# S5 mixer: the latent's norm ahead of all context states, T's loads behind the latent's operands on the DMA queue, and a new share-out of the output copies

## The chip, the cores and the metric

One core of one Trainium2 chip runs the program. The metric is the device time of one execution in microseconds; lower is better. Every time below is in microseconds unless marked ns. Engines: PE multiplies matrices, DVE and ACT do elementwise work and copies, POOL (GpSimd) helps with copies, SP issues nearly all DMA transfers.

## The reference, cut to what matters

Two layers work on 512 latent tokens `x` and 256 context tokens `ctx`, each 1024 wide, in float32. Layer 0 has an S5 mixer (a diagonal state space model in both directions, 64 groups of 16 channels and 64 states), layer 1 a GLA mixer. The context runs first and its last state starts the latent's scan.

```
for i in range(DEPTH):                                        # DEPTH = 2
    x  = ffn_half_step(x,  ...);  xc = ffn_half_step(xc, ...)
    hx = rmsnorm(x,  norm_w[i, 1]) * (1.0 + sx[4]) + sx[3]
    hc = rmsnorm(xc, norm_w[i, 1]) * (1.0 + sc[4]) + sc[3]
    yc, yx = s5_mixer(hc, hx, ...) if i == 0 else gla_mixer(hc, hx, ...)
    x = x + sx[5] * yx
    x = ffn_half_step(x, ...)                                 # and xc alike, but for the last layer
return rmsnorm(x, final_norm_w)

# s5_mixer, for each direction (backward on the flipped tokens), u = h in groups:
bu = einsum('blgc,gpc->blgp', u, bbar)                        # complex: real and imaginary half
h[t] = abar * h[t - 1] + bu[t]
y = einsum('blgp,gcp->blgc', h_re, c_re) - einsum('blgp,gcp->blgc', h_im, c_im)
# then, from both directions:
z = einsum('bld,de->ble', gelu(y_f + y_b + d_skip * h), w_glu) + b_glu
val, gate = split(z);  out = val * sigmoid(gate)
```

## The kernel before, in words

Tokens stand in the columns of transposed tiles (`xT`, 128 channels by 768 tokens, eight channel tiles `kt`). Context comes first (256 columns), then the latent (512). The code calls operations in a program order, and a planner inside the tile framework then fixes each engine's order at build time. It weighs what it expects of durations and of buffers coming free, so an edit in one place can move rows elsewhere too. On the chip each engine and each DMA queue works strictly in its order and waits by semaphores. `c.tc.issue_after(ins)` keeps what is called under it behind the named instruction.

The S5 mixer takes time in steps of 8 tokens (`L5`), so that a scan needs 32 steps for the context (`NX5`) and 64 for the latent, 96 (`N5`) in all:

- **Norm and operands.** `norm` sums squares, takes the reciprocal root on DVE (`rstd`, sums on PE at L163, small steps at L167 to L175), spreads it over the partitions on PE (`spread`, L182), scales on DVE (L201) and shifts on ACT (L788). It runs in thirds of 256 tokens. Its last third is the latent's second half. Parts of a norm are put into a queue (`later`) and let go one after the other by `tick()`, or all at once by `ensure()`. When the latent's last third is done, `put` stores it to DRAM (`s5U<-big`), and `load_u` reads it back in groups (`u<-s5U`), the operand of the states.
- **States** (`states`, matmuls at L816, evacuation at L821 by ACT or DVE). For each `kt` the operand R (tiles `rm`, and the weight slots `wraw`, `whi`, `wlo`) is multiplied by `u`. The context's matmuls have 32 columns, the latent's 64. R is stored in the weight slots that later loads use again.
- **Scan** (`scan`, L504, on DVE): two directions, for each step a product with the diagonal and two additions. The first context steps follow the context states; then latent states and scan steps are called in turn.
- **Lagged part** (`lagged`): for each `kt` a tile of T is loaded (`c.dma` at L849) into a free weight slot, reordered by ACT (L850) and multiplied by `u` on PE (L856); ACT writes the result back over `u` (L858).
- **Outputs** (`outputs`). For each `kt` the scanned states are gathered into `xs` (two buffers, by `kt % 2`): for each of two group halves four sorts of copies (L890), forward and backward, real and imaginary. A forward copy is 64 x 380 elements; a backward one comes as 64 x 124 (context) and 64 x 256 (latent) on DVE. The table at the call in `work` says which engine takes which: `copies[z][a]`, z the direction and a the half. In kt 0 and 1 the first 80 steps are copied early by ACT, and only the rest by the table. PE multiplies `xs` with the operand (L911), DVE adds the lagged part (L913), ACT applies gelu (L915); the result goes to DRAM (`s5Y`).
- **GLU** (`glu`): the result is read back (`yk`, three buffers), split into a high and a low part (`h`; ACT cast L936, DVE difference L937), and multiplied by the weights, which are split too (L88 on ACT, L89 on DVE; the three products are L113, L114 and L115). It alternates between two weights at the start, and it is followed by feed-forward layers made of the same products.

The calls in order, in `hybrid_trunk`: load the context's u and R, context states (in the loop a `tick()` each, and `ensure()` at kt 3), first scan steps, a modulation block (`ten`), latent states in turn with scan steps, the rest of the scan, `lagged`, another block, `outputs`, two blocks, the outputs' `work`, `glu`.

Of the kernel before, what the change touches and what calls it, by code (L numbers as in the profile page):

```python
# [15 lines left out]
P = 128  # L16
# [11 lines left out]
def fview(t, off, dims, p0=0, n=P):  # L28

    b = t[p0:p0 + n]  # L30
    return bass.AP(b.tensor, b.offset + off, [list(b.ap[0])] + [list(d) for d in dims])


def dview(ap, off, dims):

    return bass.AP(ap.tensor, ap.offset + off, [list(d) for d in dims])
# [432 lines left out]
C5 = 16  # L469
S5P = 64  # L470
L5 = 8
N5 = TOK // L5
# [4 lines left out]
class S5:  # L477
# [285 lines left out]
    def load_u(self, kt, kind):  # L763

        tile = (self.u[kt][:, :, :NX5], self.u[kt][:, :, NX5:])[kind]
        n = tile.shape[-1]
        self.c.dma(tile, dview(self.U[kind], kt * P * L5 * n, [(n, P), (C5 * L5 * n, 8), (1, n)]))

    def inputs(self):

# [30 lines left out]
    def states(self, kt, kind, evac):  # L801


        c, nc, r = self.c, self.c.nc, self.r
        n0, n = ((0, NX5), (NX5, N5 - NX5))[kind]
        m = (32, 64)[kind]
        u = self.u[kt][:, :, n0:n0 + n]
        banks = [c.bank() for _ in range(kind + 1)]
        for part in range(2):
            for z in range(2):  # L810
                i = (part * 2 + z) * 4 * n
                b, o = banks[i // 512], i % 512
                for q in range(4):
                    for g in range(2):
                        for p0 in range(64 * g, 64 * g + 64, m):
                            nc.tensor.matmul(b[p0:p0 + m, o + q * n:o + (q + 1) * n],  # L816
                                             self.rm[2 * kt + part][:, z * 512 + q * P + p0:z * 512 + q * P + p0 + m],
                                             u[:, 2 * q + g], start=True, stop=True)
                src = fview(b, o + z * (n - 1), [(n, 4), (1 - 2 * z, n)])
                dst = fview(r, n0 * P + part * 64 + z * 32 + 4 * kt, [(1, 4), (P, n)])  # L820
                last = (nc.scalar.copy if evac[part] else nc.vector.tensor_copy)(out=dst, in_=src)  # L821
        return last
# [20 lines left out]
    def lagged(self):  # L843

        c, nc = self.c, self.c.nc
        for kt in range(KT):
            tm = c.spare()
            c.dma(tm.rearrange("p (i x) -> p i x", i=L5), self.T[:, :, kt * P:(kt + 1) * P])
            tg = c.spare().rearrange("p (x i) -> p x i", i=L5)  # L849
            nc.scalar.copy(out=tg.rearrange("p x i -> p i x"), in_=tm.rearrange("p (i x) -> p i x", i=L5))  # L850
            for h in range(2):
                b = c.bank()
                u = self.u[kt][:, 4 * h:4 * h + 4]
                for i in range(4):
                    g = 4 * h + i
                    nc.tensor.matmul(b[:, i * N5:(i + 1) * N5], tg[:, g * C5:(g + 1) * C5].rearrange("p c i -> p (c i)"),  # L856
                                     u[:, i], start=True, stop=True)
                nc.scalar.copy(out=u.rearrange("p g n -> p (g n)"), in_=b[:, :4 * N5])  # L858

    def outputs(self, pool, ahead, yp, last):  # L860


        c, nc, r = self.c, self.c.nc, self.r
        loaded, self.ys = {}, []

        def load(kt):
            om = [c.spare() for _ in range(2)]
            for z in range(2):
                c.dma(om[z], self.O[kt][z])
            return om  # L870
        for kt in range(ahead):
            loaded[kt] = load(kt)
        xs = [pool.tile([P, 2, 8, N5], F32, name=f"xs{i}", tag=f"xs{i}", bufs=1) for i in range(2)]
        for x in xs:
            nc.gpsimd.memset(x[:, 0, :, 0:1], 0.0)
        def states(kt, s0, s1, copies):

            x = xs[kt % 2]
            nc.gpsimd.memset(x[:, 1, :, NX5 - 1:NX5], 0.0)
            for g in range(2):  # L880
                for a in range(2):
                    def move(z, lo, hi, to, step):

                        lo, hi = max(lo, s0), min(hi, s1)
                        if lo >= hi:
                            return
                        at, to = (lo, to(lo)) if step > 0 else (hi - 1, to(hi - 1))
                        src = fview(r, at * P + a * 64 + z * 32 + 4 * kt, [(1, 4), (step * P, hi - lo)], 64 * g, 64)
                        dst = fview(x, z * 8 * N5 + g * N5 + to, [(2 * N5, 4), (1, hi - lo)], 64 * a, 64)
                        copies[z][a](out=dst, in_=src)  # L890
                    move(0, 0, N5 - 1, lambda s: s + 1, 1)
                    move(1, 0, NX5 - 1, lambda s: NX5 - 2 - s, -1)
                    move(1, NX5 - 1, N5 - 1, lambda s: NX5 + N5 - 2 - s, -1)
        early = 80
        with c.tc.issue_after(last.ins):
            for kt in range(2):
                states(kt, 0, early, [[nc.scalar.copy] * 2] * 2)

        def work():
            for kt in range(KT):  # L900
                x = xs[kt % 2]
                om = loaded.pop(kt) if kt in loaded else load(kt)
                states(kt, early if kt < 2 else 0, N5, [[nc.scalar.copy, nc.gpsimd.tensor_copy], [nc.vector.tensor_copy] * 2])
                y = pool.tile([P, 8, N5], F32, tag="y5", name="y5", bufs=4)
                for h in range(2):
                    b = c.bank()
                    for i in range(4):
                        g = 4 * h + i
                        o = b[:, i * N5:(i + 1) * N5]
                        for z in range(2):  # L910
                            nc.tensor.matmul(o, om[z][:, g * P:(g + 1) * P], x[:, z, g], start=(z == 0), stop=(z == 1))  # L911
                    yh = y[:, 4 * h:4 * h + 4].rearrange("p g n -> p (g n)")
                    nc.vector.tensor_tensor(out=yh, in0=b[:, :4 * N5], op=ALU.add,  # L913
                                            in1=self.u[kt][:, 4 * h:4 * h + 4].rearrange("p g n -> p (g n)"))
                nc.scalar.activation(y, y, AF.Gelu_apprx_tanh)  # L915
                c.dma(dview(self.Y, kt * P * TOK, [(N5, P), (C5 * TOK, 8), (1, N5)]), y)
                if 0 < kt < 4:
                    self.load_y(yp, kt - 1)
        return work
# [482 lines left out]
def hybrid_trunk(tc, ins, out):  # L1402
    nc = tc.nc
    with ExitStack() as stack:
        core = Core(tc, stack)
# [6 lines left out]
        def pool(name, side=None):  # L1412
            return tc.tile_pool(name=name, bufs=1, reuse_waits="tile", side=side)
# [94 lines left out]
        with ExitStack() as norms:  # L1508
            with pool("mid", "right") as mp, ExitStack() as inner:
                box = []  # L1510

                def after(s, e):
                    if not box:
                        box.append(s5.inputs())
                    if e < TOK:
                        box[0](s, e, 7, 3)
                    else:
                        box[0](s, e, 3, 3)
                ffn(0, 0, both, halves, halves, thirds, mp, lambda: fill00(inner.enter_context(pool("s5p"))) + [
                    lambda: (inner.close(), operands00(norms))], after, 3, 5, ending)  # L1520

            with pool("s5r") as sp:
                for kt in range(KT):
                    s5.load_u(kt, 0)
                s5.load_r([sp.tile([P, UNIT], F32, tag="rm", name="rm", bufs=4) for _ in range(4)] +
                          [core.slot(i % 2, F32) for i in range(3)])
                units = [core.slot(i % 2, F32) for i in range(4)]
                ada[blocks[0]] = mods.load(*blocks[0], lambda: units.pop())
                for kt in range(KT):
                    s5.states(kt, 0, [kt % 2] * 2)  # L1530
                    core.tick()
                    if kt == 3:
                        core.ensure()
                s5.scan(sp, 0, 8)
                ten(1)
                for kt in range(KT):
                    s5.load_u(kt, 1)
                    last = s5.states(kt, 1, (0, 1))
                    s5.scan(sp, 8 + 3 * kt, 11 + 3 * kt)
# [74 lines left out]
```

## Time and profile before

| | us |
|---|---|
| median of 3 runs | 2894.43 |
| lowest and highest | 2892.82, 2896.95 |
| profiled execution, its own time | 2893.03 |
| its span, first to last instruction | 2891.3 |
| PE busy | 2732.8 |
| DVE busy | 1795.4 |
| ACT busy | 857.4 |
| POOL busy | 22.3 |
| DMA instruction packets (q8) | 143 |

PE is busy for 95% of the span. The page's picture in 40 slices of 72 us shows where it isn't: digits are tenths of the slice, and the tenth to twelfth cover the S5 mixer.

```profile
PE   6999999996569999999999999999999999799998
DVE  6699999536894565557527565665268786643433
```

A group's row gives its line, engine, operation, tiles, shapes and count, then busy time, mean ns, and the idle time ahead of it with what ended it. A timeline row gives start, length, engine, line, operation, form, count, and in brackets the idle time ahead and its releaser. "issue" there is a wait for nothing that the profile shows.

### The profile page before, as it was taken

The numbers are of one execution on the slowest core, as the hardware profiler recorded it, in microseconds if no ns is written. First come the engines' busy times: TensorE is split into PE (matmuls) and PEld (weight loads), VectorE is DVE, ScalarE is ACT, GpSimd is POOL, SyncE is SP. The second block draws the span as 40 slices with busy tenths as digits, with TensorE's granted clock in tenths as the row PEclk, the third lists the DMA queues.
The fourth block names the chain that finished last, engine by engine and source line by source line (L and its number), as shares of the span: only waits on it lengthen the run. The fifth ranks groups of instructions, "written<-read, shape, count | busy, mean of one in ns | idle before, by whom it ended". The sixth has DMA issues, their size and how long they took to land. (4 is left out here: it accounts for less than half of the span.)

```text
span 2891.3 us, 44942 instructions
## 1 busy us (share of the span) xinstructions
PE 2732.8 (95%) x18231; PEld 2581.4 (89%) x18231; DVE 1795.4 (62%) x4080; ACT 857.4 (30%) x1386; POOL 22.3 (1%) x57
## 2 busy tenths in 40 slices
PE   6999999996569999999999999999999999799998
PEld 5899999995459999999999999999988798788887
DVE  6699999536894565557527565665268786643433
ACT  4222222224363421111224221121246453332223
POOL 0000000000020000000000000000000000000000
PEclk9999999997789999999999999999999899799999
DMA  6545555526653133334211333333103112233330
GB/s 225 160 118 148 154 152 147 171 66 199 219 156 93 59 98 100 95 110 124 88 59 45 110 110 102 102 103 96 52 23 88 45 48 70 66 116 91 94 94 30
DMA packets 396044, 305.43 MB, mean 106 GB/s; under 512 B 57994, under 2 KB 344188, under 8 KB 395836
## 3 DMA queue, kind: packets, MB, share of 16 engines
q1 hardware_dynamic: 391228, 293.12, 34.7%
q10 hardware_dynamic: 4608, 9.44, 0.8%
q8 instruction: 143, 2.34, 0.3%
q14 instruction: 65, 0.53, 0.1%
HBM read 275.77 MB, written 30.41 MB: 106 GB/s over the span
## 5 line engine op out<-in xcount | busy, mean ns | idle before, releaser
L113 PE MATMUL bank<-h,whi 128*128 128x384 f32 (+3 forms) x3160 | 1044.7, 334 | 8.7 <-ACT whi L88 6.1
L114 PE MATMUL bank<-h,whi 128*128 128x384 f32 (+3 forms) x3160 | 1048.9, 333 | 0.0
L115 PE MATMUL bank<-h,wlo 128*128 128x384 f32 (+3 forms) x3160 | 1047.6, 332 | 0.0
L113 PEld LDWEIGHTS bank<-h,whi 128*128 128x128 f32 (+1 forms) x3160 | 593.9, 189 | 30.7 <-ACT whi L88 6.7
L88 ACT CAST whi<-wraw 128x1024 fp32r<-128x1024 f32 x313 | 327.4, 1048 | 966.3 <-PE bank L114 905.1
L114 PEld LDWEIGHTS bank<-h,whi 128*128 128x128 f32 (+1 forms) x3160 | 596.3, 189 | 17.2 <-issue 0.4
L115 PEld LDWEIGHTS bank<-h,wlo 128*128 128x128 f32 (+1 forms) x3160 | 595.1, 188 | 17.7 <-issue 0.7
L89 DVE TENSOR_TENSOR wlo<-wraw,whi 128x1024 fp32r<-128x1024 f32 x313 | 380.8, 1219 | 254.7 <-ACT whi L88 250.9
L114 PE MATMUL bank<-ml,whi 128*128 128x384 f32 (+2 forms) x1360 | 448.0, 330 | 0.0
L113 PE MATMUL bank<-mh,whi 128*128 128x384 f32 (+2 forms) x1360 | 445.7, 331 | 1.8 <-DVE xT L279 1.8
L115 PE MATMUL bank<-mh,wlo 128*128 128x384 f32 (+2 forms) x1360 | 446.2, 329 | 0.0
L279 DVE SCALAR_TENSOR_TENSOR xT<-bank,hg,xT 128x256 f32<-128x256 f32 (+2 forms) x488 | 221.4, 499 | 199.3 <-PE bank L115 198.8
L264 DVE TENSOR_TENSOR sg<-sg,bank 128x384 f32<-128x384 f32 (+2 forms) x166 | 89.4, 539 | 354.6 <-PE bank L115 339.2
L113 PEld LDWEIGHTS bank<-mh,whi 128*128 128x128 f32 x1360 | 256.3, 189 | 9.6 <-issue 2.8
L114 PEld LDWEIGHTS bank<-ml,whi 128*128 128x128 f32 x1360 | 256.9, 189 | 6.5 <-issue 0.4
L115 PEld LDWEIGHTS bank<-mh,wlo 128*128 128x128 f32 x1360 | 256.8, 189 | 6.2 <-issue 0.2
L427 DVE SCALAR_TENSOR_TENSOR adaacc<-wraw,cs,adaacc 128x512 f32<-128x512 f32 x336 | 236.9, 744 | 19.0 <-DMA wraw<-in_ada_w_dram 18.5
L265 ACT CAST mh<-sg 128x384 fp32r<-128x384 f32 (+2 forms) x166 | 83.5, 503 | 322.0 <-DVE sg L264 318.1
L263 ACT ACTIVATE sg<-bank 128x384 f32<-128x384 f32 (+2 forms) x166 | 79.5, 479 | 197.3 <-PE bank L115 195.1
L266 DVE TENSOR_TENSOR ml<-sg,mh 128x384 fp32r<-128x384 f32 (+2 forms) x166 | 89.8, 541 | 28.1 <-ACT mh L265 28.1
L150 ACT ACTIVATE sq<-xT 128x256 f32<-128x256 f32 (+1 forms) x126 | 52.0, 427 | 59.2 <-DVE xT L279 39.5
L201 DVE SCALAR_TENSOR_TENSOR nt<-xT,sc,bank 128x256 f32<-128x256 f32 (+2 forms) x136 | 61.8, 476 | 12.6 <-PE bank L182 9.7
(298 smaller groups left out, 2337.6 us busy)
## 6 DMA issues: line engine op xcount, KB each, us to landing
wraw<-in_ffn_w_in_dram SPq DMA_DIRECT2D x176, 512.0 KB, 4.2
wraw<-in_ada_w_dram SPq DMA_DIRECT2D x111, 512.0 KB, 4.0
wraw<-in_ffn_w_out_dram SPq DMA_DIRECT2D x88, 512.0 KB, 3.5
wraw<-in_gla_w_in_dram SPq DMA_DIRECT2D x24, 512.0 KB, 3.9
s5R<-s5r ACTq DMA_DIRECT2D x16, 512.0 KB, 4.9
s5O<-s5g SPq DMA_DIRECT2D x64, 128.0 KB, 3.8
wraw<-in_s_w_glu_dram SPq DMA_DIRECT2D x16, 512.0 KB, 6.5
big<-in_ada_w_dram SPq DMA_DIRECT2D x12, 512.0 KB, 8.8
```

Source lines behind the costliest of these rows:

```text
L88: nc.scalar.copy(out=hi[:, :n], in_=raw[:, :n])
L89: nc.vector.tensor_tensor(out=lo[:, :n], in0=raw[:, :n], in1=hi[:, :n].bitcast(F32), op=ALU.subtract)
L113: mm(out, wh, a[0], start=first, stop=False)
L114: mm(out, wh, a[1], start=False, stop=False)
L115: mm(out, wl, a[0], start=False, stop=last)
L201: nc.vector.scalar_tensor_tensor(out=t[:, a - s:z - s], in0=self.xT[:, k, a:z], scalar=sc[i][:, k:k + 1], in1=r[:, a - s:z - s], op0=ALU.m ...
L263: nc.scalar.activation(sg, banks[0][:, :e - s], AF.Silu)
L264: nc.vector.tensor_mul(sg, sg, banks[1][:, :e - s])
L265: nc.scalar.copy(out=mh[:, o], in_=sg)
L266: nc.vector.tensor_tensor(out=ml[:, o], in0=sg, in1=mh[:, o].bitcast(F32), op=ALU.subtract)
L279: nc.vector.scalar_tensor_tensor(out=self.xT[:, d, a:z], in0=banks[d][:, a - s:z - s], scalar=gate[i][:, d:d + 1], in1=self.xT[:, d, a:z], ...
L427: nc.vector.scalar_tensor_tensor(out=acc[:, v], in0=w[:, k], scalar=col, in1=acc[:, v], op0=ALU.mult, op1=ALU.add)
```

## The change

Four edits. `load_u` keeps the instruction of its last load. In `lagged` each load of T is issued behind that instruction. In `outputs` the table of copies changes: POOL takes all forward copies, ACT and DVE one half each of the backward ones. In `hybrid_trunk` the `tick()` and `ensure()` inside the loop over the context states go, and one `ensure()` is called ahead of the loop.

```diff
-        self.c.dma(tile, dview(self.U[kind], kt * P * L5 * n, [(n, P), (C5 * L5 * n, 8), (1, n)]))
+        self.loaded = self.c.dma(tile, dview(self.U[kind], kt * P * L5 * n, [(n, P), (C5 * L5 * n, 8), (1, n)]))
...
-            c.dma(tm.rearrange("p (i x) -> p i x", i=L5), self.T[:, :, kt * P:(kt + 1) * P])
+            with c.tc.issue_after(self.loaded.ins):
+                c.dma(tm.rearrange("p (i x) -> p i x", i=L5), self.T[:, :, kt * P:(kt + 1) * P])
...
-                states(kt, early if kt < 2 else 0, N5, [[nc.scalar.copy, nc.gpsimd.tensor_copy], [nc.vector.tensor_copy] * 2])
+                states(kt, early if kt < 2 else 0, N5, [[nc.gpsimd.tensor_copy] * 2, [nc.scalar.copy, nc.vector.tensor_copy]])
...
+                core.ensure()
                 for kt in range(KT):
                     s5.states(kt, 0, [kt % 2] * 2)
-                    core.tick()
-                    if kt == 3:
-                        core.ensure()
```

Line numbers of the changed kernel are one higher from L850 to about L1528 (L890 becomes L891, and so on).

PE, at the start of the context states; the last rows of the feed-forward layer are L115, and 32x32 marks context states. With - what stood there before, with + what stands there now:

```order
 L115 MATMUL bank<-mh,wlo 128x256
+L182 MATMUL bank<-ident,rs 128x128 x2
+L163 MATMUL aux<-ones,ssq 128x1 x2
+L182 MATMUL bank<-ident,rs 128x128 x2
 L816 MATMUL bank<-u,rm 32x32 x32
-L182 MATMUL bank<-ident,rs 128x128 x2
-L816 MATMUL bank<-u,wraw 32x32 x14
-L816 MATMUL bank<-u,rm 32x32 x32
-L816 MATMUL bank<-u,wraw 32x32 x2
-L163 MATMUL aux<-ones,ssq 128x1 x2
```

The sums (L163) and the last spread (the second L182) of the latent's last third stand ahead of every context state now; before, the second spread stood still further down, behind 224 of them. An order counts a matmul once where the profile, which sees two passes of a float32 matmul, counts two.

SP, at the latent's operands; s5U is the DRAM copy of the normed latent, s5T is T:

```order
+L70 DMA s5U_794<-big 128x512 x8
+L70 DMA u<-s5U_794 128x8x64 x8
 L70 DMA whi<-s5T 128x8x128
-L70 DMA s5U_794<-big 128x512 x8
-L70 DMA u<-s5U_794 128x8x64
 L70 DMA wlo<-s5T 128x8x128
-L70 DMA u<-s5U_794 128x8x64 x7
 L70 DMA wraw<-s5T 128x8x128
```

All eight stores and all eight loads of u stand ahead of the first load of T; before, one load of T stood ahead of the stores and one between the first load of u and the other seven.

ACT, at the end of the outputs and the start of the GLU, before (y_8986 is the result of kt 6, y_9026 that of kt 7):

```order
309 L936 CAST h<-yk 128x64x8
310 L915 ACTIVATE y_8986<-y_8986 128x768
311 L915 ACTIVATE y_9026<-y_9026 128x768
312 L88 CAST whi<-wraw 128x1024 x4
313 L936 CAST h<-yk 128x8x32
```

and there now:

```order
315 L937 CAST h<-yk 128x64x8
316 L88 CAST whi<-wraw 128x1024
317 L937 CAST h<-yk 128x8x32
318 L937 CAST h<-yk 128x64x8
319 L937 CAST h<-yk 128x8x32
320 L937 CAST h<-yk 128x64x8
321 L937 CAST h<-yk 128x8x32
322 L916 ACTIVATE y_9026<-y_9026 128x768
323 L937 CAST h<-yk 128x64x8
324 L88 CAST whi<-wraw 128x1024 x3
```

Six casts stood ahead of the two gelus before, and four weight casts followed at once. Now the gelu of kt 6 stands ahead of the six casts (rows 310 to 315), and one weight cast and five more casts stand between them and the gelu of kt 7; three weight casts follow a cast later. In the GLA stage of layer 1 some rows of PE, DVE and ACT change places too.

## Prediction

> **What bounds the kernel now.** First the busy time by stretch, to find where TensorE (PE), which sets the end, is not full. Columns: stretch, length, then PE, weight load, DVE, ACT and POOL busy with instruction counts, granted clock, DMA share, GB/s.
>
> ```profile
> core 0: us, PE busy (x) PEld busy (x) DVE busy (x) ACT busy (x) POOL busy (x), PEclk, DMA share, GB/s
> 666.20:674.00 7.80, 5.17 (x321) 4.42 (x318) 7.28 (x25) 6.19 (x13) 0.00 (x0) 0.98 0.84 170
> 674.00:690.00 16.00, 6.36 (x322) 5.83 (x326) 4.95 (x18) 4.91 (x13) 0.00 (x0) 0.50 1.02 371
> 690.00:703.75 13.75, 9.49 (x397) 6.52 (x389) 3.38 (x9) 7.15 (x13) 0.00 (x0) 0.60 0.34 104
> 703.75:749.50 45.75, 27.32 (x576) 25.70 (x575) 39.08 (x212) 23.97 (x27) 0.45 (x6) 0.78 0.67 176
> 876.00:960.00 84.00, 84.00 (x534) 84.00 (x533) 29.31 (x46) 20.38 (x31) 0.00 (x0) 1.00 0.22 63
> ```
>
> From 876 PE is full (84.00 of 84.00), so whatever moves the start of the gated product (GLU) moves the end. Before it the S5 mixer is a chain: context states (666 to 705), DVE's scan (to 814), outputs (to 850), GLU. In the states no engine is busy from 674 to 690. The waits on PE's timeline say why (start, length, form, count, idle before and its releaser):
>
> ```profile
> 668.83 0.61 PE L163 MATMUL aux<-ones,ssq 128*128 128x1 f32 x4
> 670.90 0.42 PE L816 MATMUL bank<-u,rm 128*32 128x32 f32 x28 [0.76 <-issue]
> 675.28 0.26 PE L816 MATMUL bank<-u,rm 128*32 128x32 f32 x1 [2.51 <-issue]
> 675.28 2.34 PE L816 MATMUL bank<-u,wraw 128*32 128x32 f32 x126
> 681.77 0.34 PE L816 MATMUL bank<-u,wraw 128*32 128x32 f32 x8 [4.15 <-issue]
> 682.03 1.22 PE L182 MATMUL bank<-ident,rs 128*128 128x128 f32 x4
> 689.07 0.64 PE L816 MATMUL bank<-u,wlo 128*32 128x32 f32 x30 [4.06 <-issue]
> 692.67 0.32 PE L816 MATMUL bank<-u,whi 128*32 128x32 f32 x4 [1.67 <-issue]
> 697.23 0.70 PE L816 MATMUL bank<-u,rm 128*32 128x32 f32 x34 [2.49 <-issue]
> 704.36 0.46 PE L816 MATMUL bank<-u,wlo 128*32 128x32 f32 x32
> ```
>
> Between the stalls that end at 675.28 and 681.77 stand 1 + 126 = 127 matmuls: with their weight loads 254 instructions. The page gives the reason for that number:
>
> ```profile
> PE 2732.8 (95%) x18231; PEld 2581.4 (89%) x18231; DVE 1795.4 (62%) x4080; ACT 857.4 (30%) x1386; POOL 22.3 (1%) x57
> q8 instruction: 143, 2.34, 0.3%
> ```
>
> 143 instruction packets of 2.34 MB / 143 = 16 KB for 2 x 18231 PE instructions make 255 per packet. So I read these stalls as PE waiting for its program: a block of about 128 matmuls, executed in under 3 us, is followed by the next only when its packet has come. A period is 681.77 - 675.28 = 6.49 and 689.07 - 681.77 = 7.30 us while DMA is at share 1.02, and 3.60 and 4.56 behind that (to 692.67 and 697.23). Does the fetch run ahead when PE waits? In the DMA view from 766 to 820, where the scan leaves PE idle for most of the time, the queues listed are
>
> ```profile
> q1 hardware_dynamic: 2170, 6.33, 30.6%
> q14 instruction: 3, 0.02, 0.1%
> ```
>
> and q8 is not among them: no packet came, so it doesn't run ahead.
> [...]
>
> **The change part by part.**
>
> *Norm ahead of the context states.* In the order of before the last spread (L182) stands behind 448 state matmuls (those in the timeline from 666.1 to 682) and their stalls: 682.03. The sums (L163) can't go earlier than 668.83, since they wait for the squares. DVE's reciprocal root ends at 677.18 + 0.16 between copies that go behind it now.
>
> ```profile
> 677.18 0.16 DVE L175 SCALAR_TENSOR_TENSOR rs<-rs 128x2 f32<-128x2 f32 x1
> 742.29 0.61 DVE L821 COPY big<-bank 128x256 f32<-128x256 f32 x1 [1.95 <-PE bank L816]
> 772.62 0.17 DVE L446 TENSOR_TENSOR mod<-aux,cols 128x8 f32<-128x8 f32 x1 [2.34 <-PE aux L406]
> ```
>
> Its twelve small steps at some 0.2 us and five L201 (0.4 each) between them take 4.6 us: spread about 674.5, 7.5 us earlier. The price: all 1,024 state matmuls are queued behind it on PE and start at 675.5 instead of 666.1. Two blocks had been executed in those 9 us, and they aren't lost to PE's speed but to the fetch, which goes on only as PE enters blocks. From 676.5 (the next block entered) eight boundaries lie ahead: (321 + 322 + 397) / 128 = 8.1 blocks. I take three at 6.9 us (mean of 6.49 and 7.30), as the latent's stores and loads, now 8 us earlier, keep DMA full to about 697, and five at 3.60: 676.5 + 20.7 + 18.0 = 715.2, against 704.36 + 0.46 = 704.8. **+10.4 us** for the start of the scan (bounds: no delay, 705; all but one at 6.9 with the last at 3.6, some 722, of which I take 720).
>
> *Latent operands ahead of T.* SP's queue of before:
>
> ```profile
> 684.67 8.43 SPq L70 DMA_DIRECT2D s5U<-big  x8
> 693.15 0.45 SPq L70 DMA_DIRECT2D u<-s5U  x1
> 702.73 0.56 SPq L70 DMA_DIRECT2D wlo<-s5T  x1
> 703.34 9.13 SPq L70 DMA_DIRECT2D u<-s5U  x7
> ```
>
> A T load that needs a buffer holds SP from 693.60 to 702.73, and seven u loads behind it go out to 712.5. In the new order they follow the stores directly: last one out by about 696, before the scan starts. What that pays is what the scan waits for. Between 703.75 and 749.50 DVE is idle 45.75 - 39.08 = 6.7 us, nearly all from 740 on, as at 742.29, since latent states lag. With u present when the scan starts they run ahead: I leave 1.5 of the 6.7 (ACT's copies of T stand between its evacuations still): **-5.2**. The wait of 2.34 at 772.62 shrinks as DVE comes later; I leave half: **-1.2**. T's own loads move behind the u loads on SP, but lag the scan less; counted at nothing, since DVE has 35 us of context scan as cover. Without that cover they cost about what ACT waits for one now:
>
> ```profile
> 733.32 2.06 ACT L850 COPY wraw<-wlo 128x1024 f32<-128x1024 f32 x1 [2.58 <-DMA wlo<-s5T]
> ```
>
> Scan end: 10.4 - 5.2 - 1.2 = **+4.0** (from -6.6 to +9).
>
> *Outputs' copies.* Rounds (kt) 2 to 7 take 840.56 - 835.53 = 5.03 us each. Two views: POOL's and DVE's timeline, and single POOL copies cut out of one round.
>
> ```profile
> 835.53 2.11 POOL L890 COPY xs<-big 64x380 f32<-64x380 f32 x2 [2.74 <-PE bank L911]
> 840.56 2.09 POOL L890 COPY xs<-big 64x380 f32<-64x380 f32 x2 [2.74 <-PE bank L911]
> 840.56 2.56 DVE L890 COPY xs<-big 64x124 f32<-64x124 f32 x4
> 843.63 1.33 DVE L890 COPY xs<-big 64x124 f32<-64x124 f32 x4
> L890 POOL COPY xs<-big 64x380 f32<-64x380 f32 x1 | 0.8, 848 | 2.7 <-PE bank L911 2.7
> L890 POOL COPY xs<-big 64x380 f32<-64x380 f32 x1 | 1.2, 1193 | 0.1
> L890 POOL COPY xs<-big 64x60 f32<-64x60 f32 x4 | 1.4, 338 | 78.3 <-DVE big L504 78.2
> ```
>
> DVE's four copies take 2.56 beside POOL and 1.33 without it, POOL's 1.193 against 0.848: they hinder each other. DVE now has one set of four (1.33), POOL four copies, so POOL becomes the bound: 4 x 0.848 + 2 x 0.345 + 0.17 (clearing and gaps) = 4.25 us. Six rounds gain 6 x 0.78 = 4.7; in kt 0 and 1 POOL does four small copies in turn instead of two: 2 x 2 x 0.338 = 1.4 lost. ACT moves as many elements as before. **-3.3**.
> [...] The 2.56, below 1.33 + 2 x 0.848 = 3.03, shows some overlap.
> Bounds: -4.7 (kt 0 and 1 hidden) and +0.3 (strictly in turn: 4 x 0.848 + 1.33 + 0.12 = 4.84, 6 x 0.19 gained, 1.4 lost).
>
> *The tail.* The planner also moved ACT's order at the last outputs. Of before:
>
> ```profile
> 847.11 4.32 ACT L936 CAST h<-yk 128x256 fp32r<-128x256 f32 x6 [0.68 <-DVE xs L890]
> 851.22 0.84 ACT L915 ACTIVATE y<-y 128x768 f32<-128x768 f32 x1
> 855.98 0.69 PE L113 MATMUL bank<-h,whi 128*128 128x384 f32 x1 [6.07 <-ACT whi L88]
> 856.93 0.69 PE L113 MATMUL bank<-h,whi 128*128 128x384 f32 x1
> ```
>
> PE's last output matmul ends at 855.98 - 6.07 = 849.91, and the second weight, from which PE runs through, comes 7.0 us behind it. In the new order the gelu of kt 6 is followed by six casts, one weight, five casts, the gelu of kt 7, a cast and only then the second weight: 0.84 + 4.32 + 0.95 + 5 x 0.72 + 0.84 + 0.72 + 0.95 = 12.2 us. The gelu of kt 6 starts about 4.25 - 1.2 = 3.1 us before PE's last matmul (a round, less the two additions), so 9.1 behind it: **+2.1** (bounds 0, if the casts go earlier, and +5, if one waits for its reload).
>
> *Behind the GLU* some rows of the GLA stage change places, on PE beside full work. Counted at nothing, with bounds of 3 us to either side, less than the longest single wait shown above.
>
> **Sum** for the profiled execution: 4.0 - 3.3 + 2.1 = +2.8. It took 2893.03 us, 2891.3 of it the span; 2895.8. The median shown, 2894.43, is 1.4 above it: **2897**.
>
> **The rivals.**
> 1. *The fetch runs ahead, or isn't what holds PE.* Then the states take what PE's clock lets them: 0.50 granted, 126 matmuls in 2.34 us, so 1,024 in 19 us; end about 695 to 700, and at least DVE's and ACT's evacuations with them. Scan start -5 to -8, waits -6.4 less what comes back as T lags (3): scan -9. Sum -9 - 3.3 + 2.1 = -10: 2884. For it: the view calls the stalls "issue", its word for a wait it can't name. Against: 127 to 128 matmuls between stalls, and no packet from 766 to 820.
> 2. *Fetch at the full price, slower.* DMA stays full behind 697 (T loads, two blocks of other weights now meet the states), so that the states end at 720: scan +9; POOL's gain as forecast or half, tail +2.1: +8 to +11, about 2904. It decides from the fifth period on: if that still lasts 6 us or more, this is the case.
> 3. *Copies strictly in turn.* Outputs +0.3 instead of -3.3, the rest as forecast: 2900 to 2901.
> That the change doesn't do what it says is no rival in the order itself, but it is for the effect: u early pays only if the scan had waited for it, and it waited 6.7 us.
>
> **How the numbers follow.** Forecast 0.45, first rival 0.2, second 0.25, third 0.1. A difference under 0.2% (5.8 us, so 2888.6 to 2900.2) is about what a measurement here can't tell from none. Faster: 0.17 of the first and 0.05 of the forecast, 0.22. Slower: 0.2 of the second, 0.06 of the third, 0.04 of the forecast, 0.3. Same: 0.48. Range 2886 to 2908: it leaves out the lower part of the first rival and ends of the second.
>
> **What the profile of after would show.** The spread near 674.5 and the first 32-column state behind it; stalls named "issue" 128 matmuls apart whose ends run on to 710 or beyond; u loads on SP directly behind the stores, out by 697; the scan's start near 715 and no wait above 1 us in 740 to 755; POOL without long waits at a round of 4.2 to 4.3 us; PE's wait ahead of the GLU split in two, the second weight 9 us behind the last output matmul. Wrong would be: states ending before 707, rounds of 4.8, or PE idle anew behind 960.

## The result and the profile after

| | before | changed |
|---|---|---|
| median of 20 runs, us | 2894.40 | 2899.23 |
| lowest and highest | 2888.74, 2897.72 | 2895.60, 2903.40 |
| ratio of times (95% interval) | | 1.0016 (1.0010 to 1.0022) |
| profiled execution, its span | 2893.03, 2891.3 | 2895.86, 2894.1 |

The change costs 4.6 us (0.0016 x 2894.4), between 3 and 6. The forecast was 2897 against 2894.43, 2.6 us slower.

The two profiled executions can't be subtracted whole. Code that is the same in both ran 3 us later in the changed kernel's execution, from about 130 us on. PE's timeline (start, length, engine, line, operation, form, count) gives a common mark, the last matmul of the feed-forward layer ahead of the context states. Before and changed:

```profile
665.87 0.28 PE L115 MATMUL bank<-mh,wlo 128*128 128x256 f32 x1
```

```profile
668.86 0.28 PE L115 MATMUL bank<-mh,wlo 128*128 128x256 f32 x1
```

**Stage times below are counted from the start of this matmul.** First the states, on PE's timeline of the changed kernel (in brackets the idle time ahead and its releaser):

```profile
671.87 0.58 PE L163 MATMUL aux<-ones,ssq 128*128 128x1 f32 x4 [2.29 <-DVE ssq L151]
677.41 1.19 PE L182 MATMUL bank<-ident,rs 128*128 128x128 f32 x4 [4.96 <-DVE rs L175]
678.53 1.08 PE L816 MATMUL bank<-u,rm 128*32 128x32 f32 x64
685.82 0.38 PE L816 MATMUL bank<-u,rm 128*32 128x32 f32 x11 [1.72 <-issue]
692.11 0.70 PE L816 MATMUL bank<-u,wraw 128*32 128x32 f32 x36 [4.19 <-issue]
696.38 0.34 PE L816 MATMUL bank<-u,whi 128*32 128x32 f32 x9 [2.17 <-issue]
701.32 0.49 PE L816 MATMUL bank<-u,wlo 128*32 128x32 f32 x19 [2.79 <-issue]
705.72 0.89 PE L816 MATMUL bank<-u,rm 128*32 128x32 f32 x43 [2.31 <-issue]
709.42 0.48 PE L816 MATMUL bank<-u,rm 128*32 128x32 f32 x18 [1.56 <-issue]
718.01 0.46 PE L816 MATMUL bank<-u,wlo 128*32 128x32 f32 x32
```

The spread stands at 677.41 - 668.86 = 8.6 us, against 682.03 - 665.87 = 16.2 before. PE waits for it with nothing else to do, and the last context state ends at 718.47 - 668.86 = 49.6 us against 38.9. Six stalls are left, 6.3, 4.3, 4.9, 4.4 and 3.7 us apart. From 664.5 to 682.5, nearly all of it ahead of the states' first stall, the DMA view of the changed kernel lists two queues, and q8, which brings PE's program (8 packets more for the 2,048 instructions more of e8), isn't one of them:

```profile
q1 hardware_dynamic: 10110, 4.86, 99.7%
q14 instruction: 1, 0.01, 0.2%
```

While PE waits for the spread, no packet comes. From 682.6 to 709.4, where the six stalls are, the view lists q8 with as many packets:

```profile
q8 instruction: 6, 0.10, 1.6%
```

In the trace each of the six stalls ends 1.3 to 1.5 us behind the end of one of these packets. SP's queue shows the other half of the edit: the u loads go out behind the stores without a T load between them, at 20.8 to 31.6 us instead of 27.3 to 46.6.

```profile
680.01 9.36 SPq L70 DMA_DIRECT2D s5U<-big  x8
689.66 10.77 SPq L70 DMA_DIRECT2D u<-s5U  x8
700.48 1.02 SPq L70 DMA_DIRECT2D whi<-s5T  x1
```

DVE's timeline gives the scan: of before its last step, of the changed kernel the first step, the only waits over 0.6 us and the last step.

```profile
813.52 0.23 DVE L504 TENSOR_TENSOR big<-big,st 128x64 f32<-128x64 f32 x1
```

```profile
717.66 0.28 DVE L504 TENSOR_TENSOR st<-s5sa,big 128x128 f32<-128x128 f32 x1
749.56 0.61 DVE L821 COPY big<-bank 128x256 f32<-128x256 f32 x1 [0.96 <-PE bank L816]
779.72 0.17 DVE L446 TENSOR_TENSOR mod<-aux,cols 128x8 f32<-128x8 f32 x1 [1.87 <-PE aux L406]
820.47 0.48 DVE L504 TENSOR_TENSOR big<-big,st 128x64 f32<-128x64 f32 x2
```

The scan starts at 717.66 - 668.86 = 48.8 us, before at 703.75 - 665.87 = 37.9: +10.9. It ends at 820.95 - 668.86 = 152.1 us, before at 813.75 - 665.87 = 147.9: +4.2. Then the outputs. PE's first matmuls of two neighbouring rounds, and POOL's and DVE's copies in one:

```profile
841.55 0.46 PE L912 MATMUL bank<-xs,whi 128*128 128x96 f32 x2 [0.22 <-POOL xs L880]
845.55 0.46 PE L912 MATMUL bank<-xs,wraw 128*128 128x96 f32 x2 [0.19 <-POOL xs L880]
```

```profile
837.52 3.77 POOL L891 COPY xs<-big 64x380 f32<-64x380 f32 x4
```

```profile
837.07 0.70 DVE L891 COPY xs<-big 64x124 f32<-64x124 f32 x2
838.39 1.29 DVE L891 COPY xs<-big 64x124 f32<-64x124 f32 x2
```

A round takes 4.00 us instead of 5.03, and POOL copies for 3.77 of it. Last the tail, ACT's timeline and PE's:

```profile
850.29 4.28 ACT L937 CAST h<-yk 128x256 fp32r<-128x256 f32 x6
855.07 1.05 ACT L88 CAST whi<-wraw 128x1024 fp32r<-128x1024 f32 x1 [0.49 <-DMA wraw<-in_s_w_glu_dram]
857.25 3.37 ACT L937 CAST h<-yk 128x256 fp32r<-128x256 f32 x5 [1.14 <-DMA yk<-s5Y]
860.41 0.85 ACT L916 ACTIVATE y<-y 128x768 f32<-128x768 f32 x1
862.02 2.97 ACT L88 CAST whi<-wraw 128x1024 fp32r<-128x1024 f32 x3
```

```profile
863.15 0.69 PE L113 MATMUL bank<-h,whi 128*128 128x384 f32 x1 [10.29 <-ACT whi L88]
```

PE's last output matmul ends at 863.15 - 10.29 = 852.86, so at 184.0 us, as before (849.91 - 665.87 = 184.0): the outputs have given back the 4.2 us of the scan. The GLU, though, waits 10.29 us instead of 6.07, for a cast that begins at 862.02: +4.2. It starts at 194.3 us instead of 190.1.

So +4.2 at the start of the GLU, and +4.6 in the medians. The profiled execution shows less at its end, because behind the GLU's start it takes 2894.1 - 863.15 = 2031.0 us against 2035.3. Of that, 2.7 us come from one place. A stretch of PE's feed-forward work in which the matmuls of both kernels stand in the same order (columns as in the prediction; clock third from last), before and changed:

```profile
1545.00:1625.00 80.00, 77.66 (x637) 77.50 (x636) 48.07 (x129) 32.16 (x63) 0.00 (x0) 0.96 0.19 54
```

```profile
1545.00:1625.00 80.00, 77.39 (x659) 77.15 (x658) 49.80 (x136) 31.55 (x64) 0.00 (x0) 1.00 0.14 42
```

The granted clock was 0.96 in one and 1.00 in the other. In the profiles of the kernel before and of the ten experiments this part takes 2033.1 to 2037.6 us, so I read 2031.0 as a lucky draw and not as a gain of the change.

### The profile page after: what moved, and what is told of

Read it like the earlier page. It is cut to its first block, busy times and chain, and to the rows that moved or that the text cites. A ratio compares the mean times of both kernels' runs of the same rounds, so it can differ in the third digit from the quotient of the medians.

```text
span 2894.1 us, 44943 instructions
## 1 busy us (share of the span) xinstructions
PE 2729.7 (94%) x18231; PEld 2577.8 (89%) x18231; DVE 1788.1 (62%) x4052; ACT 859.3 (30%) x1398; POOL 32.7 (1%) x73
## 3 DMA queue, kind: packets, MB, share of 16 engines
q8 instruction: 143, 2.34, 0.3%
## 5 line engine op out<-in xcount | busy, mean ns | idle before, releaser
L115 PE MATMUL bank<-h,wlo 128*128 128x384 f32 (+3 forms) x3160 | 1045.3, 332 | 0.0
L113 PEld LDWEIGHTS bank<-h,whi 128*128 128x128 f32 (+1 forms) x3160 | 592.8, 188 | 34.5 <-ACT whi L88 10.9
L115 PEld LDWEIGHTS bank<-h,wlo 128*128 128x128 f32 (+1 forms) x3160 | 593.1, 188 | 17.7 <-issue 0.7
L115 PE MATMUL bank<-mh,wlo 128*128 128x384 f32 (+2 forms) x1360 | 446.1, 329 | 0.0
L115 PEld LDWEIGHTS bank<-mh,wlo 128*128 128x128 f32 x1360 | 256.6, 189 | 6.3 <-issue 0.2
```

Source lines behind the costliest of these rows:

```text
L113: mm(out, wh, a[0], start=first, stop=False)
L115: mm(out, wl, a[0], start=False, stop=last)
```

## The experiments

Ratios are to the kernel before, run beside each on the same chip. The table has, from the trace of each run, the start of the last context state, of the last scan step, of PE's last output matmul and of its first GLU matmul, in us behind the mark, and the ratio with its 95% interval.

| run | states | scan | outputs | GLU | ratio |
|---|---|---|---|---|---|
| before | 38.8 | 147.6 | 183.8 | 190.1 | |
| changed | 49.4 | 151.9 | 183.7 | 194.3 | 1.0016 (1.0010 to 1.0022) |
| e1 norm alone | 51.1 | 156.4 | 191.7 | 198.1 | 1.0018 (1.0009 to 1.0027) |
| e2 copies alone | 40.2 | 149.9 | 180.8 | 189.9 | 0.9997 (0.9988 to 1.0006) |
| e3 norm in the middle | 41.9 | 147.9 | 179.2 | 188.7 | 0.9989 (0.9980 to 0.9997) |
| e4 T's loads alone | 38.7 | 146.2 | 181.8 | 188.2 | 0.9997 (0.9988 to 1.0006) |
| e5 changed, new tail | 51.0 | 153.4 | 184.8 | 190.5 | 1.0008 (1.0000 to 1.0017) |
| e6 changed, block's loads late | 50.4 | 152.3 | 183.2 | 194.4 | 1.0018 (1.0008 to 1.0027) |
| e7 middle, T as before, new tail | 39.0 | 144.4 | 175.4 | 181.7 | 0.9975 (0.9964 to 0.9986) |
| e8 changed, states doubled | 77.6 | 188.1 | 219.5 | 231.4 | one run, 2934.19 us |
| e9 middle, T as before | 36.3 | 141.4 | 172.2 | 180.2 | 0.9979 (0.9970 to 0.9989) |
| e10 as e7, weights held | 38.9 | 144.6 | 175.6 | 178.7 | 0.9972 (0.9961 to 0.9982) |

### e1: the norm alone

```diff
+                core.ensure()
                 for kt in range(KT):
                     s5.states(kt, 0, [kt % 2] * 2)
-                    core.tick()
-                    if kt == 3:
-                        core.ensure()
```

> The kernel before with the one edit that lets the norm go ahead of the context states; copies and T loads as before (the order of SP then has the u loads directly behind the stores by itself). Theory A (the PE program is fetched a block ahead only, as PE enters blocks, so the states that start 9 us later end some 10 us later): first 32-column state some 9.5 us behind the feed-forward layer's end, fetch stalls 128 matmuls apart, scan starts some 10 us later than before, its waits for the latent fall from 6 to about 1 us, scan end +4 us; outputs' rounds 5.0 us; gap ahead of the GLU 6 us as before; total +4 us (+0.14%). Theory B (early u pays, the states' delay is hidden, and the measured loss comes from the tail alone): scan end -4 us, total -4 us.

Median 2898.78 against 2892.97, +5.2 us by the ratio. The states end 12.3 us later and the scan starts some 11 us later; the gap ahead of the GLU is as before (198.1 - 191.7 = 6.4). Theory B falls: this edit by itself loses what the whole change loses. It lost more in the scan than expected: one wait, for the modulation block (L446), was 5.42 us here, against 2.34 before and 1.87 in the changed kernel.

### e2: the copies alone

```diff
-[[nc.scalar.copy, nc.gpsimd.tensor_copy], [nc.vector.tensor_copy] * 2]
+[[nc.gpsimd.tensor_copy] * 2, [nc.scalar.copy, nc.vector.tensor_copy]]
```

> The kernel before with the new table of copies alone. Its ACT order at the end has one weight cast and two casts of the read-back between the six casts and the gelu of kt 7, and three weight casts behind it. Theory A (the new copies gain 4 us in the rounds and the planner's new order of the tail gives most of it back): scan end unchanged, rounds 4.0 us, PE's last output matmul -4 us, gap ahead of the GLU 7 to 8 us instead of 6, total -2.5 us (-0.1%). Theory B (tail gives back nothing; whatever the changed kernel lost came from the norm): total -4 to -5 us. Theory C (POOL and DVE strictly in turn): rounds 4.8 us, total 0 to +2 us.

From the last scan step to the last output matmul 30.9 us instead of 36.2, with rounds of 4.0 us; theory C falls. The GLU's gap is 8.87 us instead of 6.07, so 2.8 go back. Median 2892.57 against 2892.97: -0.9 us by the ratio, with an interval from -3.5 to +1.7. Theory A's -2.5 lies inside, and so does no gain at all; theory B's -4 to -5 does not.

### e3: the norm in the middle

The changed kernel, but with

```diff
-                core.ensure()
                 for kt in range(KT):
                     s5.states(kt, 0, [kt % 2] * 2)
+                    if kt == 1:
+                        core.ensure()
```

> The changed kernel, but with the norm let go after the second of the eight groups of context states (the loop calls ensure at kt 1) instead of ahead of all. PE has then 128 context matmuls of the order (256 of the profile, two blocks) to do while DVE works on the reciprocal root. Theory A (cost is blocks not entered while PE waits): first state starts with the feed-forward layer's end as before, scan starts within 2 us of before, u loads on SP are out some 5 us earlier than before, waits of the scan near 1 us, scan end -4 us; rounds 4.0 us (-4 us), tail +1 to +2 us; total -6 us (-0.2%). Theory B (the early norm is what matters and the states' position does not): like the changed kernel or slower, +2 to +5 us.

-3.2 us by the ratio where -6 was expected. The first state follows the feed-forward layer at once, the spread comes as early as in the changed kernel (9.8 us for its last matmul, against 9.3), and the last state at 41.9 instead of 49.4. So what costs is indeed how many states stand behind the spread, not the early norm. But the scan stood still once more. DVE's timeline, and ACT's:

```profile
705.94 0.29 DVE L504 TENSOR_TENSOR st<-s5sa,big 128x128 f32<-128x128 f32 x1 [3.32 <-ACT big L821]
```

```profile
703.67 2.02 ACT L851 COPY wlo<-whi 128x1024 f32<-128x1024 f32 x1 [3.65 <-DMA whi<-s5T]
705.49 0.41 ACT L821 COPY big<-bank 128x128 f32<-128x128 f32 x1
```

ACT's queue has its first copy of T ahead of an evacuation of context states, and T's load is now behind all u loads: ACT waits 3.65 us for it, and the scan waits for ACT. In the changed kernel the states are late enough to hide that. The other thing to see: the last u load goes out at 30.8 us, nearly as early as in the changed kernel (29.2), yet the scan's waits at 77 to 85 us are still 0.51 + 1.47 + 1.01 = 3.0, of 5.5 before.

### e4: T's loads alone

```diff
-        self.c.dma(tile, ...)
+        self.loaded = self.c.dma(tile, ...)
...
-            c.dma(tm..., self.T[:, :, kt * P:(kt + 1) * P])
+            with c.tc.issue_after(self.loaded.ins):
+                c.dma(tm..., self.T[:, :, kt * P:(kt + 1) * P])
```

> The kernel before with the loads of T put behind the last load of u, and nothing else; PE's order of the states is that of before. Theory A (u loads held up by a T load cost the scan its waits at 740 to 750): u loads out on SP by about 703 instead of 712, scan starts as before, waits 2 to 4 us less, scan end -3 us, total -3 us (-0.1%). Rival (latent states lag for ACT's copies of T, which now come later still): waits as before or 2 us more, total 0 to +2 us.

The u loads are out 10 us earlier (the last at 35.5 instead of 45.8), the waits behind the context scan are 1.17 + 1.28 + 0.96 = 3.4 us instead of 5.5, and the scan ends 1.4 us earlier in its profile. The ratio, -0.9 us (-3.5 to +1.7), doesn't tell that from nothing. So by the waits u's lateness was worth some 2 us, not the 5 that I had put on it.

### e5: another tail

The changed kernel with the GLU's first two weights called ahead of the read-back, and its casts from the second tile on behind the second weight's cast:

```diff
+        ws = [[c.weight(wg[:, :, q * D:q * D + P]) for q in range(2)]]
+        first = c.cast                       # set in parts: self.cast = nc.scalar.copy(out=hi..., in_=raw...)
         for k in range(KT):
...
-                nc.scalar.copy(out=h, in_=src)
+                with ExitStack() as late:
+                    if k >= 1:
+                        late.enter_context(c.tc.issue_after(first.ins))
+                    nc.scalar.copy(out=h, in_=src)
```

> The changed kernel with another order at the start of the GLU: its first two weights are called ahead of the read-back, and the casts of the read-back from the second channel tile on are issued behind the second weight's cast. ACT then has two casts and one weight between the gelus of kt 6 and kt 7, and the two first weights right behind the latter. All ahead of PE's last output matmul is that of the changed kernel. Theory A (the planner's order of ACT costs the GLU's start 4 us): gap between PE's last output matmul and its first GLU matmul 3 to 5 us instead of 10.3, total 5 to 7 us below the changed kernel, so -1 to 0 us against before. Theory B (the gap only hides a wait that comes out again, for instance for the last read-back): gap shorter, but PE waits anew within the next 20 us, total as the changed kernel, +4 to +5 us.

Between the theories. PE's timeline:

```profile
857.25 0.69 PE L113 MATMUL bank<-h,whi 128*128 128x384 f32 x1 [5.43 <-ACT whi L88]
872.35 0.44 PE L114 MATMUL bank<-h,whi 128*128 128x384 f32 x1 [0.23 <-DVE h L943]
880.01 0.98 PE L113 MATMUL bank<-h,whi 128*128 128x384 f32 x4 [1.63 <-ACT h L942]
```

The gap fell from 10.29 to 5.43 us, and 2.2 us came back as waits for the read-back (0.23, 1.63, and 0.38 at 873.88). The ratio fell from 1.0016 to 1.0008, some 2.3 us, about the difference of the two; but the two intervals overlap, so the medians alone don't show this step. By the trace the tail's order is a real cost, and nearly half of it is only moved when it is mended.

### e6: less traffic beside the states

The changed kernel with the loads of the next modulation block moved:

```diff
-                ada[blocks[0]] = mods.load(*blocks[0], lambda: units.pop())
...
                 for kt in range(KT):
                     s5.load_u(kt, 1)
+                with tc.issue_after(s5.loaded.ins):
+                    ada[blocks[0]] = mods.load(*blocks[0], lambda: units.pop())
+                ten(1)
```

> The changed kernel, but the four 512 KB loads of the next modulation block, which go out while the context states run, are put behind the latent's u loads. PE's matmuls and their order in the states stay. Theory A (program packets of PE queue behind data transfers): fetch periods between 676 and 697 shrink from 4.9 to 6.3 us towards 4, the u loads are out some 4 us earlier, the context states end 2 to 4 us earlier, total 1 to 3 us below the changed kernel. Rival (the states are bound by PE's clock of 0.50 or by their evacuation, not by the fetch): end of the states unchanged within 1 us.

A miss: the u loads are out 2.4 us earlier, but the last state is at 50.4 us as in the other runs with the norm first (49.4 to 51.1), and the ratio is 1.0018. The traffic had only moved, and met a later fetch. PE's timeline at that place, where the block's loads now are:

```profile
697.94 0.89 PE L816 MATMUL bank<-u,rm 128*32 128x32 f32 x43 [2.30 <-issue]
704.65 0.48 PE L816 MATMUL bank<-u,rm 128*32 128x32 f32 x18 [4.58 <-issue]
```

The same period in the changed kernel, from 705.72 to 709.42, has 127 matmuls as well. Busy time by stretch, with the DMA share next to last, of e6 and of the changed kernel:

```profile
697.94:704.65 6.71, 2.13 (x127) 1.99 (x127) 1.14 (x3) 0.74 (x2) 0.00 (x0) 0.50 0.92 309
```

```profile
705.70:709.40 3.70, 2.14 (x127) 2.00 (x127) 1.14 (x3) 0.76 (x2) 0.00 (x0) 0.50 0.02 5
```

Same matmuls, same clock, same copies on DVE and ACT: 6.71 us at a DMA share of 0.92, 3.70 at 0.02. That shows theory A's link between traffic and period. By the end of the states, the mark that had been set for this run, it doesn't tell the theories apart.

### e8: the states' instructions doubled

Each matmul of the context states is issued twice, so that the same values are written again.

```diff
+                            for _ in range(2 - kind):
-                            nc.tensor.matmul(b[p0:p0 + m, ...], ..., start=True, stop=True)
+                                nc.tensor.matmul(b[p0:p0 + m, ...], ..., start=True, stop=True)
```

> The changed kernel with each matmul of the context states issued twice (the second writes the same values again): 1,024 more matmuls, 2,048 more instructions, 8 more packets; no other transfer and no other evacuation. Theory A (the fetch sets the pace): from the first to the last state 39.7 us in the changed kernel, now 8 periods of about 4 us more, 70 to 75 us, and stalls still about 128 matmuls apart. Rival (pace set by PE at clock 0.50, 126 matmuls in 2.3 us, or by the evacuations): 40 to 59 us, without stalls at 128.

This one tells them apart by its mark. First and last row of the states on PE's timeline, and two periods between them:

```profile
676.31 1.76 PE L817 MATMUL bank<-u,rm 128*32 128x32 f32 x108
694.42 2.31 PE L817 MATMUL bank<-u,wraw 128*32 128x32 f32 x127 [2.57 <-issue]
698.52 2.31 PE L817 MATMUL bank<-u,wraw 128*32 128x32 f32 x128 [1.78 <-issue]
743.53 0.86 PE L817 MATMUL bank<-u,wlo 128*32 128x32 f32 x64
```

The page's line for PE's program, against 143 packets:

```profile
q8 instruction: 151, 2.47, 0.4%
```

2,048 more instructions made 8 more packets. From first to last state it is 67.9 us instead of 39.7, that is 28.2 / 8 = 3.5 us for a packet's worth, though PE executes such a block in 2.3 us (127 matmuls at 694.42) and then stands still. No transfer and no evacuation was added. It is a little under theory A's 70 to 75 (the added periods were 3.5 us, not 4), and well beyond the rival's 59.

### e7, e9, e10: the parts put together

e9 is e3 without the edit on T's loads; e7 adds to e9 the tail of e5; e10 adds to e7 that no other GLU weight is cast ahead of the first two:

```diff
-        self.cast = nc.scalar.copy(out=hi[:, :n], in_=raw[:, :n])
+        with ExitStack() as late:
+            if self.hold:                    # first.ins, for all other weights of the GLU
+                late.enter_context(self.tc.issue_after(self.hold))
+            self.cast = nc.scalar.copy(out=hi[:, :n], in_=raw[:, :n])
```

> Norm let go after the second group of context states, T loads as before the change, the new table of copies, and the new order at the GLU's start. Theory A: in the run with the norm in the middle the scan waited 3.3 us behind its start for ACT, whose queue stood at a copy of T that had been put behind the u loads; without that edit this wait goes, and the GLU's gap falls from 9.5 to 3 to 5 us: 4 to 6 us below that run, -7 to -9 us against before (-0.25 to -0.3%). Rival (the tail's gain comes back as PE waits for the read-back, the wait for T moves on): -3 us as that run.

> Norm let go after the second group of context states and the new table of copies; the loads of T and the start of the GLU as the planner puts them. It splits the gain of the run with the norm in the middle and the new tail (-7.8 us against before). Theory A (the edit on T's loads costs the scan's start about 3 us when the states aren't late, as ACT waits for T with an evacuation of a context state behind it): no wait above 1 us in the first 5 us of the scan, scan end 2 to 4 us earlier than in the run with that edit, GLU gap 9 to 9.5 us, total -5 to -6.5 us. Rival (the whole difference came from the tail): scan end as in the run with the edit, total -3 to -4 us.

> The run with the norm in the middle and the new tail, with one more rule: no other GLU weight is cast ahead of the first two. There the fourth weight's cast stood ahead of the gelu of kt 7 and waited 4.3 us for its load, with the gelu and both first weights queued behind it. Theory A (head of ACT's queue sets the GLU's start): gap between PE's last output matmul and the first GLU matmul 3 to 4 us instead of 6.1; PE may wait 1 to 3 us anew for the last read-back, which comes 2.4 us earlier at best; total 0 to 3 us below that run, -8 to -11 us against before. Rival (the last read-back, not the weights, is now what the GLU waits for): gap shorter, the same time lost at the last channel tile, total within 1 us of that run.

e9 came out at -6.1 us by the ratio, as theory A had it: without the edit on T the wait of 3.3 us is gone (the scan's first steps wait 0.42 and 0.33 us), and its waits at 74 to 78 us are 1.8. Its scan ends 6.5 us earlier than e3's, more than the 2 to 4 that were expected; the context states end earlier too, by 5.6 us. Its GLU gap, 7.73 us, is below the expected 9. e7 came out at -7.2, inside its range; its gap is 6.06 and not 3 to 5, since ACT's queue holds another weight's cast, waiting 4.30 us for its load, ahead of the gelu of kt 7. In e10 that order is mended, and PE's timeline has

```profile
845.30 0.69 PE L117 MATMUL bank<-h,whi 128*128 128x384 f32 x1 [2.85 <-ACT whi L92]
867.99 0.97 PE L117 MATMUL bank<-h,whi 128*128 128x384 f32 x4 [0.68 <-ACT h L946]
```

The gap is 2.85 us, and the wait for the last read-back 0.68. Yet the median is 2885.43, against 2886.08 for e7: the rival's line, within 1 us. The read-back's wait explains 0.3 of the 3 us that went missing (0.68 against 0.41 in e7); the rest isn't explained. e7, e9 and e10 can't be told from one another by their intervals. All three beat both kernels; e10, with the lowest ratio, is 8.1 us (5 to 11) faster than before.

## Why the prediction came out right, step by step

In time from the mark, prediction and profile of the changed kernel against before:

| step | predicted | measured |
|---|---|---|
| spread | -7.5 | -7.6 |
| end of the context states | +10.4 | +10.7 |
| scan's end | +4.0 | +4.2 |
| outputs' own part | -3.3 | -4.2 |
| tail | +2.1 | +4.2 |
| start of the GLU | +2.8 | +4.2 |
| whole kernel | +2.6 on the median | +4.6 (3 to 6) |

**The fetch** carried the sign, and it held: no packet while PE waited for the spread, stalls 127 matmuls apart up to the last one (709.42), the doubled states at 3.5 us for a packet. With periods guessed as three of 6.9 and five of 3.60 the sum came within 0.3 us. The single periods were not those: 6.3, 4.3, 4.9, 4.4, 3.7. So the mechanism was right, and that the sum met the end this closely is luck. Since the first rival lived on a fetch that runs ahead, it falls. The empty queue alone wouldn't settle that, as the prediction took it to from 766 to 820: a fetch that had run many blocks ahead would stand still as well. What settles it is the first stall, the one that ends at 685.82: only 181 of the 1,024 state matmuls had run by then. The second rival didn't come about: from the second period on all stayed under 5 us.

**The scan's gain was right in size and wrong in its reason.** The prediction put -5.2 us on "u present when the scan starts". In the profile the waits fell from 5.5 to about 1 us at that place, and from 2.34 to 1.87 at the modulation block. But with u nearly as early and the scan starting 3.6 us later than before (e3) 3.0 of 5.5 us stay, and T's edit alone (e4) takes 2.1 away. So about 2 to 2.5 us belong to early u. The rest I put down to the scan's own delay, as the latent states and ACT's copies of T have 11 us more to get ahead of it; no run shows this apart. That part is no gain, it only softens the loss. About 0.7 us is no wait at all: between the scan's first and last step DVE made eight copies into `xs` before (1.8 us) and four in the changed kernel (1.1 us), which is the new table's doing. And "T's own loads ... counted at nothing" was true only under that delay: e3 pays 3.3 us for them.

**The outputs** were mis-sized by 0.9 us. The round was put at 4.25 us and is 4.00. POOL's four copies take 3.77, where 4 x 0.848 + 2 x 0.345 = 4.08 was reckoned, and DVE's pair 1.29 beside POOL's copies against 0.70 at 837.07, most of it ahead of them. The third rival had POOL and DVE copying strictly in turn, which no run had shown. Added up from whole copies of before, that made a round of 4.84; it is 4.00, so this rival falls as a sum.

That the one holds the other up doesn't fall with it. Single copies, from POOL's and DVE's timeline of the changed kernel, and the same DVE copy by itself, before:

```profile
838.55 0.86 POOL L891 COPY xs<-big 64x380 f32<-64x380 f32 x1
838.61 1.07 DVE L891 COPY xs<-big 64x256 f32<-64x256 f32 x1
843.84 0.44 DVE L890 COPY xs<-big 64x256 f32<-64x256 f32 x1
```

DVE's copy begins 0.06 us behind POOL's and ends 0.27 us behind it. All eight copies of this shape that begin during one of POOL's in the changed kernel take 1.05 to 1.08 us and end 0.26 or 0.27 us behind it. So I read these eight as waiting for POOL's copy to end; what holds them up, no run shows. What made the rival's sum too high is the price for POOL: its next copy, at 839.48, takes 0.93 us instead of 0.85, so a DVE copy of 0.44 us costs POOL 0.1; where both begin together, at 834.12, POOL's takes 1.15.

**The tail** is the term that was mis-sized most, 2.1 against 4.2. The prediction took the weight cast ahead of the gelu of kt 7 for the first that the GLU needs. It is the fourth: ACT waits for its load, the last of the four that SP had issued by then (848.95), and DVE makes its low part behind those of three others. PE's first GLU matmul therefore waits for the cast at 862.02, behind the gelu, and PE enters the second weight at 864.09, 11.2 us behind its last output matmul, where 9.1 was forecast. The wrong reading is worth one cast more ahead of the second weight, about 1 us. The larger part is ACT's two waits, 0.49 us for that early weight and 1.14 for a read-back, which only the bound of +5 had allowed for; smaller differences take 0.5 back. e2 shows that it is the copies' edit that brings an order of this kind. In e5 the mended order shortened the gap by 4.9 us and brought 2.2 back as waits; the ratio's step of 2.3 us is not clear of the intervals.

**Behind the GLU** nothing was put into the sum, and nothing of size is shown: start of the GLU +4.2, median +4.6.

## What to carry to other kernels

When PE is fed with many tiny matmuls, its program can be what it waits for, as here, with stalls 127 matmuls apart and 3.5 us for each packet that e8 added: look for stalls that the profile can't name, count the instructions between them, and don't let PE wait in front of such a stretch: here no packet came while it did, and the states ended 10.7 us later. Take an early step off the critical path only as far as there is other work to put beside it: here the norm in the middle of the states got nearly as early operands for 7.5 us less delay. And when a planner orders the engines, read which buffer an operation that moved belongs to before pricing the move: a cast ahead of the others is of use only if it is the one that is waited for. Nor could two engines that hinder each other be priced here by adding up their copies (4.84 us a round, against 4.00 measured): look at single ones to see what a turn costs the engine that sets the pace.

## What was not expected of the hardware

In e8 a block of PE's program took 3.6 us to follow the one before it even with hardly a transfer on the queues: from the stall that ends at 703.55 to the one that ends at 736.23 it is nine blocks in 32.68 us. That is 1.6 times the 2.21 us that PE took for the 127 matmuls at 717.94. The mean granted clock was 0.52 there. The row is e8's, from 703 to 740:

```profile
703.00:740.00 37.00, 23.00 (x1244) 20.19 (x1244) 3.84 (x10) 4.53 (x11) 0.00 (x0) 0.52 0.02 5
```

1,244 matmuls are 9.7 blocks in 37 us, 3.8 each with the modulation block's first matmuls among them, at a DMA share of 0.02.

At the same place of the same code, between 1545 and 1625, the granted clock was 0.96 in the one profiled execution and 1.00 in the other. The second got 22 matmuls further in the same 80 us (659 against 637), worth 2.7 us, more than half of the effect that was to be measured.
